# Moving the second half's weight loads ahead of the spill stores, with a lead of three steps

## The chip, the core and the metric

The kernel runs on one core of one Trainium2 chip. The metric is the device time of one execution in microseconds; the median of three runs is compared. A profile of a single execution, taken by the hardware profiler, goes with it. PE is the matmul engine (TensorE), PEld its weight loads, DVE is VectorE, ACT is ScalarE, POOL is GpSimd and SP is SyncE, the engine whose queue issues the DMAs here.

## The reference

One layer of a hybrid decoder, for one sequence of 1024 tokens and a model width of 2048, in float32. What matters for this change is its opening:

```python
mod = silu(c) @ w_ada + b_ada                   # w_ada: 2048 x 6144
shift, scale, gate = split(mod, 3)
h = rms_norm(x, norm_gain) * (1.0 + scale) + shift
proj = h @ w_in                                 # w_in: 2048 x 8192
q_sb, k_sb, v_sb, z_sb, q_r, k_r, v_r, z_r = split(proj)
# group A: stick-breaking attention on q_sb, k_sb, v_sb, times silu(z_sb)
# group B: chunkwise retention on rotary q_r, k_r and v_r, group norm, times silu(z_r)
out = x + gate * (concat(group A, group B) @ w_out)
```

Each group has 8 heads of 128. `mod` is itself a product of a vector with a matrix of 2048 x 6144, so w_ada has to be read as a whole.

## The kernel before

**Numbers.** A float32 factor is cut into a high part in a reduced format and the rest (`split`, `split_to`, lines 168 to 181: ACT writes the high part, DVE the low one). A product is then three matmuls (`mm3`, lines 183 to 186). PE is the engine that works all the time.

**The stages.** The opening (up to about 235 us) computes the modulation and the normed h, projects the retention queries `q_r` of seven heads with it, and builds from h the factors that the main products use. Then come the large products of h with the other columns of w_in, in blocks of a Winograd scheme, with the attention and retention of finished heads between them, and at last the product with w_out. The change is in the opening alone.

**The opening's two halves.** The sequence is cut into two halves of 512 tokens. Each half has 16 steps, one for each block of 128 rows of the model width. A step `p` of a half does, in the order in which PE is given it (`start_mm`, lines 717 to 725): for each of the 7 heads three matmuls that add the product of the step's weights and the step's h to that head's PSUM tile `first`. Between the heads stand, for later steps: the transposes of x (`x_turn`, 542), which fill a PSUM tile of tag `"C"` that ACT or DVE copies to `xT`; `make_h` (593), which makes the high and low part of h on ACT and DVE; `cut_w` (705), which cuts the next weights; `ada_sums` (563) and `ada_mod` (579), which work on one chunk of 256 columns of w_ada. Transposes, sums and mods all use the tag `"C"`, of which there is one buffer. So a transposed tile must have been copied out before a sum or a mod can start. The chunk numbers 8 to 15 of w_ada give `shift`.

In the second half step `p` transposes x and makes h for step `p + 2`, and cuts the weights of step `p + 2` at heads 4 and 6. In even steps it takes `ada_mod(cc)` at head 3, in odd steps `ada_sums(cc + 1)` at head 4, with `cc = 8 + p // 2`. From step 2 on, `factors` puts work on a list of which `pieces` gives a part after most heads to ACT and DVE: pieces `whole`, `high`, `minus`, `over`, `low` make factors `B22`, `T1`, `T2`, `T3`, `T4`, `B21` of two blocks k, and `low` stores the finished `B22`, `T1` and `T2` (high and low part, `store`, 359 to 362) to DRAM.

**Between the halves.** When the first half's products are done, `spill` (873) takes each head's `first` out of PSUM: DVE multiplies it with the row of norms, and SP stores it to `rqraw` (line 881). Seven heads make seven stores.

**The order of work.** From line 872 on every engine runs in the order in which the code issues; before it only PE does. All these DMAs are issued on SP, in order. A DMA that waits, for its data or for its buffer, holds all DMAs behind it.

**Buffers.** All tiles of 128 x 512 lie in 92 buffers, which `Slots` (57) gives out in turn: the buffer that was given back first is given out first. Giving back (`put`) happens in the code's order, so a tile may get a buffer whose last reader hasn't run yet; its writer then waits for that reader, or for the store that reads it.

**Loads.** `load_w(p, hf)` (696) issues two loads (128 x 512 and 128 x 384) for step `p`; `load_ada(cc)` (501) issues eight of 256 KB. In the first half, steps 14 and 15 load the weights of the second half's steps 0 and 1. In the second half, step `p` first issues the weights of step `p + 2`, and in even steps chunk `cc + 2` of w_ada; from step 12 on it also loads blocks of w_in for the next stage (`load_raw`, 254).

Of the kernel before, what the change touches and what calls it, by code (L numbers as in the profile page):

```python
# [20 lines left out]
KC = D // P  # L21
# [35 lines left out]
class Slots:  # L57
# [21 lines left out]
    def get(self, name, cls=None, dtype=F32, borrow=False):  # L79
        assert self.free, (name, cls, self.used)  # L80
        if cls in ("raw", "ring") and self.share and not (borrow or self.loose):
            assert self.used.get(cls, 0) < self.share[cls], (name, cls, self.used)
        i = self.free.popleft()
        self.used[cls] = self.used.get(cls, 0) + 1
        t = self.pool.tile([P, HALF], dtype, tag=f"s{i}", name=name)
        self.of[id(t)] = (t, i, cls)
        return t

    def put(self, *tiles):
        for t in tiles:  # L90
            _, i, cls = self.of.pop(id(t))
            self.used[cls] -= 1
            self.free.append(i)
# [3 lines left out]
def layer_kernel(ctx, tc, x, c, w_ada, b_ada, norm_gain, w_in, sb_q_gain, sb_k_gain, ret_norm_gain, w_out,  # L97
# [156 lines left out]
    def load_raw(gi, q, block, hh, borrow=False):  # L254
        col = groups[gi][q][0] + (P if block[1] == "2" else 0) if q < 4 else single
        kc = (8 if block[2] == "2" else 0) + 4 * hh
        t = raws[gi, q, block, hh] = get(f"{block}_{gi}_{q}_{hh}", "raw", borrow=borrow)
        nc.sync.dma_start(t.rearrange("p (k n) -> p k n", n=P), w_in_k[:, kc:kc + 4, col:col + P])
# [198 lines left out]
    def prepare_entry(j):  # L457
        if j < len(entries):
            lefts[j] = left(*entries[j])
        else:  # L460
            cut_left(j - len(entries))
# [39 lines left out]
    def load_ada(cc, gs=range(8)):  # L501

        col = (D + CHUNKS1[cc] * 2 * P) if cc < 8 else CHUNKS[cc - 8] * 2 * P
        for g in gs:
            ada[cc, g] = ar = get(f"ada_{cc}_{g}")
            nc.sync.dma_start(ar.rearrange("p (j n) -> p j n", n=2 * P),
                              ada_rows[:, 2 * g:2 * g + 2, col:col + 2 * P])
# [34 lines left out]
    def x_turn(p, g, tag, bufs):  # L542

        kc = (KCS if g else KCS1)[p]
        xT[kc, g] = get(f"xT{kc}_{g}")
        tp = ps.tile([P, HALF], F32, tag=tag, bufs=bufs, name=f"xtp_{kc}_{g}")
        for t in range(4):
            src = xt[4 * g + t, kc // 4]
            nc.tensor.transpose(tp[:, t * P:(t + 1) * P], src[:, (kc % 4) * P:(kc % 4 + 1) * P], ident)
        left_in[kc // 4, g] -= 1  # L550
        if left_in[kc // 4, g] == 0:
            put(*[xt.pop((4 * g + t, kc // 4)) for t in range(4)])
        if p % 2 and g == 0:
            nc.vector.tensor_copy(xT[kc, g], tp)
        else:
            nc.scalar.activation(xT[kc, g], tp, AF.Copy)
# [6 lines left out]
    def ada_sums(cc):  # L563


        ap_ = ps.tile([P, 256], F32, tag="C", name=f"accp_{cc}")
        for j in range(16):
            g = j % 4
            nc.tensor.matmul(ap_[32 * g:32 * g + 32, :], silu_z[:, j, :],  # L569
                             ada[cc, j // 2][:, (j % 2) * 256:(j % 2) * 256 + 256], start=j < 4, stop=j >= 12)  # L570
        put(*[ada.pop((cc, g)) for g in range(8)])
        acc = get(f"acc_{cc}")
        nc.vector.tensor_copy(acc[:, 0:256], ap_)
        return acc
# [4 lines left out]
    def ada_mod(cc, acc):  # L579

        mod = ps.tile([P, 2], F32, tag="C", name=f"mod_{cc}")
        for s in range(2):
            nc.tensor.matmul(mod[:, s:s + 1], acc[:, s * P:(s + 1) * P], ones[:, 0:1], start=True, stop=True)
        put(acc)
        k0 = 2 * (CHUNKS1[cc] if cc < 8 else CHUNKS[cc - 8])
        k2 = slice(k0, k0 + 2)
        if cc < 8:
            nc.vector.tensor_tensor(mods[:, k2], mod, scale_b1[:, k2], op=ALU.add)
            nc.vector.tensor_tensor(mods[:, k2], mods[:, k2], gain_c[:, k2], op=ALU.mult)
        else:  # L590
            nc.vector.tensor_tensor(shift[:, k2], mod, shift_b[:, k2], op=ALU.add)

    def make_h(p, hf):

        kc = (KCS if hf else KCS1)[p]
        a, xT_kc = mods[:, kc:kc + 1], xT[kc, hf]
        h_hi[kc, hf] = get(f"h_hi{kc}_{hf}", None, F32R)
        nc.scalar.activation(h_hi[kc, hf], xT_kc, AF.Copy, scale=a)
        h_lo[kc, hf] = get(f"h_lo{kc}_{hf}", None, F32R)
        nc.vector.scalar_tensor_tensor(h_lo[kc, hf], xT_kc, a, h_hi[kc, hf].bitcast(F32),  # L600
                                       op0=ALU.mult, op1=ALU.subtract)
# [85 lines left out]
    def pieces(n=1):  # L687
        for _ in range(n):
            if background:
                for fn in background.popleft():  # L690
                    if fn:
                        fn()
# [3 lines left out]
    def load_w(p, hf):  # L696
        raw = []
        for i in range(2):
            n = min(HALF, NZ * P - i * HALF)
            raw.append(get(f"wr_{p}_{hf}_{i}"))  # L700
            col, kc = rqcol + i * HALF, (KCS if hf else KCS1)[p]
            nc.sync.dma_start(raw[i][:, 0:n], w_in[0][kc * P:(kc + 1) * P, col:col + n])
        return raw

    def cut_w(p, hf, raw, i):
        return split(raw[i], f"first_{p}_{hf}_{i}", min(HALF, NZ * P - i * HALF))
# [10 lines left out]
    def start_mm(p, hf, ws, heads):  # L717
        kc = (KCS if hf else KCS1)[p]
        for h in heads:
            if p == 0:  # L720
                tag, bufs = starter_tags[h]
                first[h] = ps.tile([P, HALF], F32, tag=tag, bufs=bufs, name=f"first_{h}_{hf}")
            hi, lo = ws[h // 4]
            sl = slice(h % 4 * P, (h % 4 + 1) * P)
            mm3(first[h], hi[:, sl], lo[:, sl], h_hi[kc, hf], h_lo[kc, hf], p == 0, p == KC - 1)
# [96 lines left out]
    rawz = {}  # L822
# [50 lines left out]
    def spill(h, hf):  # L873
        zt = get(f"zt_{h}_{hf}")
        if hf == 0:
            nc.vector.tensor_tensor(zt, first[h], norm_row, op=ALU.mult)
        elif h % 2:
            nc.vector.tensor_copy(zt, first[h])
        else:
            nc.scalar.activation(zt, first[h], AF.Copy)  # L880
        nc.sync.dma_start(rqraw[h][:, halves(hf)], zt)
        put(zt)

    for h in range(NZ):
        spill(h, 0)

# [2 lines left out]
    def scale_some(n):  # L889
        for _ in range(min(n, len(unscaled))):  # L890
            t = xT[unscaled.popleft(), 0]
            nc.vector.tensor_tensor(t, t, norm_row, op=ALU.mult)
            if not unscaled:
                put(norm_row)

    early = deque([("A12", hh, q) for hh in range(2) for q in range(5)])
    for p in range(KC):
        cc = 8 + p // 2
        if p + 2 < KC:
            rawz[p + 2] = load_w(p + 2, 1)  # L900
        if p % 2 == 0 and cc + 2 < 16:
            load_ada(cc + 2)
        if p >= 12:
            for _ in range(3):
                if early:
                    b, hh, q = early.popleft()
                    load_raw(0, q, b, hh)
        w, cuts = ws.pop(p), []
        heads = range(NZ) if p < KC - 1 else (3, 0, 1, 2, 4, 5, 6)
        for i, h in enumerate(heads):  # L910
            start_mm(p, 1, w, (h,))
            if p == 1 and i or p > 1 and i < 2:
                scale_some(1)
            if i == 0 and p + 2 < KC:
                x_turn(p + 2, 1, "C", 1)
            if i == 2 and p + 2 < KC:
                make_h(p + 2, 1)
            if i == 3 and p % 2 == 0:
                ada_mod(cc, sums.pop(cc))
            if i == 4 and p % 2 and cc < 15:  # L920
                sums[cc + 1] = ada_sums(cc + 1)
            if i == 3 and p % 4 == 2:
                factors((KCS[p - 2], KCS[p - 1]))
            if i in (4, 6) and p + 2 < KC:
                cuts.append(cut_w(p + 2, 1, rawz[p + 2], i // 2 - 2))
            if i not in (2, 4):
                pieces()
            if p == KC - 1:
                if i:
                    spill(heads[i - 1], 1)  # L930
                if i in (1, 3, 5):
                    prepare_entry(i // 2)
        put(h_hi.pop((KCS[p], 1)), h_lo.pop((KCS[p], 1)))
        if p + 2 < KC:
            ws[p + 2] = cuts
            put(*rawz.pop(p + 2))
# [991 lines left out]
```

## Time and profile before

| | us |
|---|---|
| median of 3 runs | 1884.33 |
| lowest and highest run | 1883.38 and 1884.34 |
| the profiled execution | 1884.66 |
| its span, first to last instruction | 1882.9 |
| PE busy | 1866.6 |
| DVE busy | 1341.8 |
| ACT busy | 826.1 |

The span is what the profile's rows add up to; the time around it, 1.8 us, is not seen in them. All times in rows are counted from the start of the span. The granted clock of PE is full over the whole span. A row of a timeline has the start, the duration, the engine, the line of the code, the operation, what it writes and reads, and in brackets how long the engine was idle before it and what ended that. A row of a window has the stretch, its length, the busy time of PE, PEld, DVE, ACT and POOL with the number of instructions, PE's clock, the share in which the DMA engines were busy, and GB/s. A row of a wait has who waited for whom, the total, the number and the longest, and the row of landings gives the shortest, median and longest time from a DMA's issue to the arrival of its data. SPq is SP's queue.

### The profile page before, as it was taken

The numbers are of one execution on the slowest core, as the hardware profiler recorded it, in microseconds if no ns is written. First come the engines' busy times: TensorE is split into PE (matmuls) and PEld (weight loads), VectorE is DVE, ScalarE is ACT, GpSimd is POOL, SyncE is SP. The second block draws the span as 40 slices with busy tenths as digits, with TensorE's granted clock in tenths as the row PEclk, the third lists the DMA queues.
The fourth block names the chain that finished last, engine by engine and source line by source line (L and its number), as shares of the span: only waits on it lengthen the run. The fifth ranks groups of instructions, "written<-read, shape, count | busy, mean of one in ns | idle before, by whom it ended". The sixth has DMA issues, their size and how long they took to land.

```text
span 1882.9 us, 29009 instructions
## 1 busy us (share of the span) xinstructions
PE 1866.6 (99%) x9565; PEld 1540.5 (82%) x9565; DVE 1341.8 (71%) x2601; ACT 826.1 (44%) x1559; POOL 82.6 (4%) x278
## 2 busy tenths in 40 slices
PE   8999999999999999999999999999999999999998
PEld 5777788888888888888888888888888888888887
DVE  3568776666768677877688676977585666596669
ACT  3647762233544454445443554334334455342231
POOL 0000000000110010001010101000000000000000
PEclk9999999999999999999999999999999999999999
DMA  9979999998698789978997988999997963994594
GB/s 317 361 240 313 319 348 370 374 359 300 209 315 299 242 285 310 305 272 264 321 317 263 305 276 290 302 304 290 308 317 253 265 214 113 359 366 163 187 313 164
DMA packets 414451, 541.04 MB, mean 287 GB/s; under 512 B 34142, under 2 KB 210648, under 8 KB 414300
## 3 DMA queue, kind: packets, MB, share of 16 engines
q1 hardware_dynamic: 413436, 538.78, 86.9%
q8 instruction: 75, 1.23, 0.3%
q14 instruction: 76, 0.62, 0.1%
q10 hardware_dynamic: 864, 0.40, 0.1%
HBM read 453.03 MB, written 86.02 MB: 286 GB/s over the span
## 4 chain that ended last, share of the span: by engine, by line
PE 92%; DVE 4%; DMA 3%; issue 1%; ACT 0%; SPq 0%; DVEq 0%; ACTq 0%
PE pj L184 19%; PE pj L186 19%; PE pj L185 19%; PE y L185 5%; PE y L184 5%; PE y L186 5%; PE first L184 3%; PE first L186 2%; PE first L185 2%; PE accp L569 1%; PE tp_B L1248 1%; PE oT L184 1%; PE oT L186 1%; PE oT L185 1%; DMA ada<-in_w_ada_dram 1%; PE zp L186 1%
## 5 line engine op out<-in xcount | busy, mean ns | idle before, releaser
L173 DVE TENSOR_TENSOR wl<-A,wh 128x512 fp32r<-128x512 f32 x392 | 270.1, 690 | 211.5 <-ACT wh L171 198.1
L171 ACT ACTIVATE wh<-A 128x512 fp32r<-128x512 f32 x392 | 247.6, 632 | 387.0 <-PE pj L185 369.8
L387 ACT ACTIVATE c<-pj 128x512 f32<-128x512 f32 x112 | 66.7, 600 | 147.4 <-PE pj L186 137.4
L294 DVE TENSOR_TENSOR A<-A,A 128x512 f32<-128x512 f32 x160 | 110.0, 693 | 1.7
L390 DVE TENSOR_TENSOR c<-pj,c 128x512 f32<-128x512 f32 x112 | 74.9, 687 | 47.9 <-PE pj L186 47.5
L1212 ACT ACTIVATE om<-zp,y 128x128 f32<-128x128 f32 (+2 forms) x96 | 55.9, 582 | 107.4 <-PE zp L186 67.2
L184 PE MATMUL first<-h_hi,wh_first 128*128 128x512 f32 x224 | 94.6, 422 | 0.1
L1228 DVE TENSOR_TENSOR_SCAN om<-om 128x128 f32<-128x128 f32 (+2 forms) x96 | 93.5, 974 | 1.1
L184 PE MATMUL pj<-T1h,wh 128*128 128x512 f32 x232 | 94.2, 406 | 0.0
L184 PE MATMUL pj<-B22h,wh 128*128 128x512 f32 x232 | 92.8, 400 | 0.0
L184 PE MATMUL pj<-B21h,wh 128*128 128x512 f32 x232 | 92.0, 397 | 0.0
L184 PE MATMUL pj<-B11h,wh 128*128 128x512 f32 x232 | 91.4, 394 | 0.0
L186 PE MATMUL pj<-T1h,wl 128*128 128x512 f32 x232 | 90.7, 391 | 0.0
L186 PE MATMUL pj<-B22h,wl 128*128 128x512 f32 x232 | 90.6, 391 | 0.0
L185 PE MATMUL pj<-T1l,wh 128*128 128x512 f32 x232 | 90.5, 390 | 0.0
L185 PE MATMUL pj<-B21l,wh 128*128 128x512 f32 x232 | 90.5, 390 | 0.0
L186 PE MATMUL pj<-B21h,wl 128*128 128x512 f32 x232 | 90.4, 390 | 0.0
L186 PE MATMUL pj<-B11h,wl 128*128 128x512 f32 x232 | 90.4, 390 | 0.0
L185 PE MATMUL pj<-B11l,wh 128*128 128x512 f32 x232 | 90.4, 390 | 0.0
L185 PE MATMUL pj<-B22l,wh 128*128 128x512 f32 x232 | 90.4, 390 | 0.0
L184 PE MATMUL pj<-T3h,wh 128*128 128x512 f32 x224 | 89.6, 400 | 0.0
L184 PE MATMUL pj<-T4h,wh 128*128 128x512 f32 x224 | 89.5, 400 | 0.0
(411 smaller groups left out, 4963.2 us busy)
## 6 DMA issues: line engine op xcount, KB each, us to landing
A<-in_w_in_dram SPq DMA_DIRECT2D x228, 256.0 KB, 5.7
ada<-in_w_ada_dram SPq DMA_DIRECT2D x120, 256.0 KB, 5.6
wB<-in_w_out_dram SPq DMA_DIRECT2D x112, 256.0 KB, 5.3
gr<-in_w_ada_dram SPq DMA_DIRECT2D x64, 256.0 KB, 5.6
T2h<-fac_T SPq DMA_DIRECT2D x56, 256.0 KB, 5.4
T2l<-fac_T SPq DMA_DIRECT2D x56, 256.0 KB, 5.4
T1h<-fac_T SPq DMA_DIRECT2D x56, 256.0 KB, 5.4
T1l<-fac_T SPq DMA_DIRECT2D x56, 256.0 KB, 5.3
```

The lines of the kernel that those rows point to most:

```text
L171: nc.scalar.activation(hi[:, 0:n], src[:, 0:n], AF.Copy)
L173: nc.vector.tensor_tensor(lo[:, 0:n], src[:, 0:n], hi[:, 0:n].bitcast(F32), op=ALU.subtract)
L184: nc.tensor.matmul(o, a_hi, b_hi, start=first, stop=False, skip_group_check=on)
L185: nc.tensor.matmul(o, a_hi, b_lo, start=False, stop=False, skip_group_check=on)
L186: nc.tensor.matmul(o, a_lo, b_hi, start=False, stop=last, skip_group_check=on)
L294: nc.vector.tensor_tensor(r[o], r[a], r[b], op=ALU.add if n == 1 else ALU.subtract)
L387: nc.scalar.activation(t, o, AF.Copy)
L390: nc.vector.tensor_tensor(dst[q, cc], o, dst[q, cc], op=ALU.add)
L569: nc.tensor.matmul(ap_[32 * g:32 * g + 32, :], silu_z[:, j, :], ada[cc, j // 2][:, (j % 2) * 256:(j % 2) * 256 + 256], start=j < 4, stop=j ...
L1212: nc.scalar.activation(om[:, :n], zp[:, :n], AF.Sigmoid, scale=y[:, 16 + i:17 + i])
L1228: nc.vector.tensor_tensor_scan(rev, rev, rev, init, op0=ALU.mult, op1=ALU.bypass)
L1248: nc.tensor.transpose(banks_[j // 2][:, c0:c0 + P], be[:, j * P:(j + 1) * P], ident)
```

## The change

The loads of the second half's steps 2 and 3 and chunk 10 of w_ada are issued ahead of the seven spill stores of the first half, and the loop then issues the weights of step `p + 3` and, in odd steps, chunk `cc + 3`. Each of these loads stands one step earlier than before in SP's order. The number of loads, what they load, and all work of the other engines stay as they are; which of the 92 buffers a tile gets changes for the tiles of the second half.

```diff
@@ -881,6 +881,11 @@
         nc.sync.dma_start(rqraw[h][:, halves(hf)], zt)
         put(zt)
 
+
+    for p in (2, 3):
+        rawz[p] = load_w(p, 1)
+        if p == 2:
+            load_ada(10)
     for h in range(NZ):
         spill(h, 0)
 
@@ -896,10 +901,10 @@
     early = deque([("A12", hh, q) for hh in range(2) for q in range(5)])
     for p in range(KC):
         cc = 8 + p // 2
-        if p + 2 < KC:
-            rawz[p + 2] = load_w(p + 2, 1)
-        if p % 2 == 0 and cc + 2 < 16:
-            load_ada(cc + 2)
+        if p and p + 3 < KC:
+            rawz[p + 3] = load_w(p + 3, 1)
+        if p % 2 and cc + 3 < 16:
+            load_ada(cc + 3)
         if p >= 12:
             for _ in range(3):
                 if early:
```

## The prediction

> **What bounds the kernel now.** I read the page first: the busy times of the engines.
>
> ```profile
> span 1882.9 us, 29009 instructions
> PE 1866.6 (99%) x9565; PEld 1540.5 (82%) x9565; DVE 1341.8 (71%) x2601; ACT 826.1 (44%) x1559; POOL 82.6 (4%) x278
> ```
>
> PE is busy for all but 16.3 us of the span. An edit that moves loads takes no matmul away, so it can win only what PE idles, and only where those loads are the cause. The next view is therefore the list of PE's waits, first for 0 to 240 us, then for the rest of the span.
>
> ```profile
> PE xtp L549 <- DMA x<-in_x_dram: 3.3, 7, 0.9
> PE mod L583 <- ACT xT L556: 1.6, 1, 1.6
> ```
>
> ```profile
> PE tp_B L1248 <- DVE al L1273: 0.9, 3, 0.4
> ```
>
> The columns are total, times and longest, in us. The waits for x lie in the first half, which the change doesn't touch, and those at L1248 lie after 500 us, in attention. One wait lies in the opening's second half: 1.6 us before the products of ada_mod. The timelines of PE, ACT and DVE around it say why.
>
> ```profile
> 139.34 0.60 PE L549 MATMUL xtp<-ident,x 128*128 128x128 f32 x4
> ...
> 141.61 0.39 PE L186 MATMUL first<-h_hi,wl_first 128*128 128x512 f32 x1
> 143.60 0.61 PE L583 MATMUL mod<-ones,acc 128*128 128x1 f32 x4 [1.61 <-ACT xT L556]
> ```
>
> ```profile
> 137.96 0.42 DVE L573 COPY acc<-accp 128x256 f32<-128x256 f32 x1
> ```
>
> ```profile
> 140.66 0.63 ACT L171 ACTIVATE wh_first<-wr 128x512 fp32r<-128x512 f32 x1 [5.04 <-DMA wr<-in_w_in_dram]
> 142.54 0.52 ACT L171 ACTIVATE wh_first<-wr 128x384 fp32r<-128x384 f32 x1 [1.24 <-DMA wr<-in_w_in_dram]
> 142.97 0.58 ACT L556 ACTIVATE xT<-xtp 128x512 f32<-128x512 f32 x1
> ```
>
> This is step p=2. Its transposes (139.34) go into the only PSUM buffer of tag C. ada_mod of the same step needs that buffer, so it needs ACT's copy xT. ACT works in order, and ahead of that copy stand the two cuts of the weights for step 3, which wait for their load until 142.5. So the load is the cause. Why it is late is in SyncE's timeline, its wait list and the windows.
>
> ```profile
> 105.18 2.47 SPq L702 DMA_DIRECT2D wr<-in_w_in_dram  x4
> 121.97 6.86 SPq L881 DMA_DIRECT2D rqraw<-zt  x7
> ...
> 129.92 4.22 SPq L506 DMA_DIRECT2D ada<-in_w_ada_dram  x8
> 134.51 2.74 SPq L702 DMA_DIRECT2D wr<-in_w_in_dram  x4
> 137.51 6.63 SPq L506 DMA_DIRECT2D ada<-in_w_ada_dram  x8
> ```
>
> ```profile
> SPq L881 <- DVE zt L876: 18.0, 7, 13.9
> ```
>
> ```profile
> 112.00:122.00 10.00, 10.00 (x74) 7.42 (x73) 4.20 (x8) 3.21 (x6) 0.00 (x0) 1.00 0.01 2
> 129.00:147.00 18.00, 16.39 (x103) 12.43 (x103) 9.26 (x18) 6.07 (x11) 0.00 (x0) 1.00 1.05 336
> ```
>
> ```profile
> DMA to landing us min/median/max: 6.0/6.6/7.1
> ```
>
> SyncE issues the loads of steps 0 and 1 until 107.65, then stands 13.9 us at the first spill store, which waits for DVE, which waits for the end of the first half on PE. Behind it stand the loads of steps 2 and 3. In 112 to 122 us the DMA engines are 1% busy; from 129 on they are full at 336 GB/s, and the weights of steps 3 and 4 (issued from 134.51) take 6.0 to 7.1 us to land, which is the last row.
>
> **The change part by part.** *The loads ahead of the stores.* Twelve loads (4 of weights, 8 of w_ada) move past the seven stores. They now follow 107.65 directly, if their buffers are free. Slots hands out 92 buffers from a queue, first freed, first used again. I walked its gets and puts in the order of the code, with the moved loads in their new places. The twelve then get buffers last used by squares of x, by chunk 7 of w_ada and by h of step 12.
>
> ```profile
> 102.78 1.93 PE L569 MATMUL accp<-ada,silu_z 128*32 128x256 f32 x32
> ```
>
> ```profile
> 104.06 0.62 ACT L514 ACTIVATE junk<-x 128x512 f32<-128x512 f32 x1
> ```
>
> The two named readers are done by 104.7, and step 12 of the first half ends before its successor's transposes, around 109. At the slowest pace of the rows above (6.63 us for eight, 0.83 each) the twelve are issued by 117.6 and landed by 124.7. The stores, due at 121.97, are not delayed: 4.3 us of cover. Were it gone, SyncE alone would be late: nothing in the opening reads what they store, and their buffers come round again only in step 3's loads. Step 3's weights are first cut about 135, so ACT waits for neither cut, copies xT at about 139.9 to 140.5, and ada_mod's acc is there at 138.4. PE ends the matmul before at 142.0, so nothing is late and **the 1.61 us go**. I find no second wait behind: 1.5 us lie between that copy and PE's need.
>
> *Three steps' lead in the loop.* No load is added; each stands one step earlier in SyncE's program. Between 129 and 146 us the engines stay full as now, but each weight tile is now issued a step or more ahead of its cut. After 144 PE waits for nothing in this stretch, so an earlier load gains nothing more.
>
> *What it costs.* Ten buffers more (2 + 8) are held during odd steps. By the walk the queue's lowest filling in steps 7 to 11 goes from 12 to 9, and in step 9 from 19 to 9. Buffers are used again sooner. From step 14 on every get falls on the same predecessor as before, so all that comes after the opening is unchanged. And in steps 7 and 9 ten loads now stand in SyncE's program ahead of stores of factors that stood ahead of them: T2 of k=1 in step 7; T1 and T2 of k=2 in step 9. Who waits for those stores? By the walk, in step 8, ACT's T2h and DVE's B22l take the two buffers of T2 of k=1. In step 10, DVE's T2 takes the buffer of T1h, ACT's T3h that of T1l, ACT's h_hi that of T2h, DVE's h_lo that of T2l. Behind h_lo on DVE stands `shift`, which frees the buffer C for the transposes of step 11. The rows:
>
> ```profile
> 161.35 1.87 SPq L702 DMA_DIRECT2D wr<-in_w_in_dram  x4
> 163.28 4.24 SPq L506 DMA_DIRECT2D ada<-in_w_ada_dram  x8
> ...
> 174.05 0.32 SPq L361 DMA_DIRECT2D fac_T<-T1l  x1
> ...
> 185.93 0.34 SPq L361 DMA_DIRECT2D fac_B<-B22l  x1
> ...
> 187.33 0.38 SPq L360 DMA_DIRECT2D fac_T<-T1h  x1
> ...
> 188.88 0.98 SPq L361 DMA_DIRECT2D fac_T<-T2l  x1
> 189.95 1.50 SPq L702 DMA_DIRECT2D wr<-in_w_in_dram  x2
> 191.50 4.84 SPq L506 DMA_DIRECT2D ada<-in_w_ada_dram  x8
> ```
>
> ```profile
> DMA to landing us min/median/max: 4.4/4.8/5.2
> ```
>
> ```profile
> 184.18 0.62 ACT L608 ACTIVATE T2h<-T 128x512 fp32r<-128x512 f32 x1
> ```
>
> ```profile
> 185.21 0.68 DVE L615 TENSOR_TENSOR B22l<-xT,B22h 128x512 fp32r<-128x512 f32 x1
> ...
> 194.47 0.69 DVE L641 TENSOR_TENSOR T<-xT,xT 128x512 f32<-128x512 f32 x1
> ...
> 195.82 0.75 DVE L600 SCALAR_TENSOR_TENSOR h_lo<-xT,mods,h_hi 128x512 fp32r<-128x512 f32 x1
> 196.49 0.15 DVE L591 TENSOR_TENSOR shift<-mod,cols 128x2 f32<-128x2 f32 x1
> ```
>
> ```profile
> 199.16 0.60 PE L549 MATMUL xtp<-ident,x 128*128 128x128 f32 x4
> ```
>
> These are SyncE's timeline, the landing of stores, and the timelines of ACT, DVE and PE. The landing row is that of the four fac_T stores of 187.33 to 188.88. Ten loads take 5.1 us (161.35 to 167.52 is twelve) to 6.3 us (189.95 to 196.34 is ten). All engine times below are 1.6 us earlier than the rows.
>
> Step 7: T1l is issued at 172.45, ten loads end at 177.9 to 179.1, the T2 stores land 4.7 later, T2h at 182.6 to 183.8, T2l half a us after. ACT wants T2h's buffer at 182.6 and DVE the other at 183.6: waits of 0 to 1.2 and 0 to 0.7 us, in front of no PE need. They may delay B22l's store by some 0.4 us.
>
> Step 9: B22l's store at 184.3 + 0.4, ten loads from 185.1, so T1h at 190.2 to 191.4, T2l 1.55 later (187.33 to 188.88) at 191.8 to 192.95, landed at 196.2 to 198.15, middle 197.2. DVE meets its first such wait at 192.9 and can start h_lo only at 197.2; shift ends 0.83 later (195.82 to 196.64), at 198.0. PE's transposes are due at 197.55. So PE waits 0.5 us, between 0 and 1.4, and up to 2.0 with step 7's delay whole. h_lo itself is needed only in step 12, some 6 us on; wl for step 12 then comes at about 199.5, also in time. I take 0.5.
>
> The fixed price of a store is where a page speaks. The Trainium skill, DMA: Bandwidth & Descriptors, section Anatomy of one DMA, fits a transfer on the GpSimd path as 2.0 us plus its bytes over 436 GB/s; for 256 KB that is an estimate of 2.6 us, and by it the T2l store would land by 195.6, before anyone is late. The trace agrees only for stores on empty queues, the first row here, not for those behind loads:
>
> ```profile
> DMA to landing us min/median/max: 2.0/2.0/2.0
> ```
>
> These are the seven spill stores; 4.4 to 5.2 us, the row above, is the nearer case.
>
> **Sum.** -1.6 + 0.5 = -1.1 us. The profiled execution took 1884.66 us, its span and 1.8 around it, and would take 1883.55; it lies 0.3 above the median of the three runs, 1884.33, so the median should be about 1883.2. About 0.2% (3.8 us) is what a measurement of this kernel can tell from no change; the whole gain at stake is below half of that.
>
> **The rivals.** *Nothing is given back.* The delayed stores land on nearly idle queues, in the spill stores' 2.0 us: T2l at 193.8 to 195, and h_lo finds its buffer free. Then the whole 1.6 stays: 1882.7. For it: the stores come at the end of ten loads, with none behind. Against it: the four stores at 187.33 had a similar load burst before them and took 4.4 to 5.2. The fit cited above would have it so.
>
> *Slower: the recycled buffers in step 10.* If the ten loads go at the full queue's 0.75 us (134.51 to 137.51 is four) and the stores behind them take the 7.1 us of step 3's weights, T2l is issued at 185.7 + 7.5 + 1.55 = 194.75 and lands at 201.85; shift ends at 202.7, and PE's transposes wait 5.1 us: a net +3.5, 1887.8. It decides against the change once T2l lands after 198.3, for then the wait passes 1.6. For it: DVE, ACT and SyncE are all in order and chained here. Against it: the burst of step 9 starts on a queue that holds only two stores and two loads.
>
> *The lead does nothing.* If a buffer of the twelve is held longer than I counted, SyncE stops there and the loads leave after the stores as now, or another ACT task takes the place of the cuts: 1884.3. Against it: all three kinds of readers end before 109.
>
> **How the numbers follow.** The forecast, 55%; nothing given back, 25%; slower, 12%; no effect, 8%. The runs shown spread over 1.0 us, half of which I add below 1882.7, and a little: low 1882.0. Above, no effect and the cheaper part of the slower case reach 1885.5. Faster by over 0.2% needs 3.8 us, which PE doesn't idle here: 0.02. Slower by over 0.2% needs a wait of 5.4 us, the far end of the slower case and what I may have missed: 0.05. The rest, 0.93.
>
> **What would show it.** In the profile after: twelve loads on SyncE right after 107.65 and ahead of the L881 stores; DMA busy in 112 to 122; no wait of PE at L583 near 142; PE's second half ending 1 to 1.6 us earlier. Of the cost: SyncE's T1 and T2 stores of k=2 after an eight-load row of w_ada near 190, DVE idle before `T` of L641 near 193 and before h_lo near 197, and a PE wait at xtp near 198 on DVE's shift of about 0.5 us. The forecast is wrong if PE shows several waits above 1 us between 145 and 225, or if anything differs after 240 us.

## The result, and the profile after

The changed kernel is slower: a median of 1890.11 us (1888.98 to 1892.34, 6 runs) against 1883.94 us (1883.18 to 1884.34, 6 runs), a ratio of 1.0031 with a 95% interval of 1.0021 to 1.0041. The forecast of 1883.2 with its range to 1885.5 was wrong. The page of the changed kernel's profile begins so:

```profile
span 1888.8 us, 29030 instructions
PE 1868.8 (99%) x9565; PEld 1543.2 (82%) x9565; DVE 1341.4 (71%) x2601; ACT 824.9 (44%) x1559; POOL 82.1 (4%) x278
```

The span is 5.9 us longer with as many matmuls, and PE is busy 2.2 us longer. PE's waits between 100 and 235 us (who waited for whom, total, times, longest):

```profile
PE xtp L549 <- DVE shift L591: 5.6, 1, 5.6
```

The 1.6 us at ada_mod are gone, as forecast. In their place stands one wait, at the place where the forecast had put one of 0.5 us. First the part that worked, SyncE's timeline and the DMA engines at the border of the halves:

```profile
106.52 3.90 SPq L702 DMA_DIRECT2D wr<-in_w_in_dram  x6
110.86 4.59 SPq L506 DMA_DIRECT2D ada<-in_w_ada_dram  x8
115.80 1.08 SPq L702 DMA_DIRECT2D wr<-in_w_in_dram  x2
122.03 6.86 SPq L881 DMA_DIRECT2D rqraw<-zt  x7
```

```profile
112.00:122.00 10.00, 10.00 (x73) 7.42 (x72) 4.20 (x8) 3.27 (x6) 0.00 (x0) 1.00 0.90 298
```

The twelve loads leave by 116.9 in the gap that was empty (DMA share 0.90 where it was 0.01), and the stores begin at 122.03, as before. Now step 9 on SyncE, and what follows on DVE, ACT and PE:

```profile
186.42 0.33 SPq L361 DMA_DIRECT2D fac_B<-B22l  x1
186.84 0.88 SPq L702 DMA_DIRECT2D wr<-in_w_in_dram  x2
187.81 4.50 SPq L506 DMA_DIRECT2D ada<-in_w_ada_dram  x8
192.40 0.46 SPq L360 DMA_DIRECT2D fac_T<-T1h  x1
193.64 0.34 SPq L361 DMA_DIRECT2D fac_T<-T1l  x1
...
195.08 0.32 SPq L361 DMA_DIRECT2D fac_T<-T2l  x1
```

```profile
DMA to landing us min/median/max: 7.8/7.8/7.8
```

```profile
185.70 0.69 DVE L615 TENSOR_TENSOR B22l<-xT,B22h 128x512 fp32r<-128x512 f32 x1 [2.17 <-DMA fac_T<-T2l]
...
200.33 0.69 DVE L641 TENSOR_TENSOR T<-xT,xT 128x512 f32<-128x512 f32 x1 [7.13 <-DMA fac_T<-T1h]
...
202.98 0.15 DVE L591 TENSOR_TENSOR shift<-mod,cols 128x2 f32<-128x2 f32 x1
```

```profile
185.13 0.63 ACT L608 ACTIVATE T2h<-T 128x512 fp32r<-128x512 f32 x1 [2.61 <-DMA fac_T<-T2h]
...
200.93 0.63 ACT L608 ACTIVATE T3h<-T 128x512 fp32r<-128x512 f32 x1 [8.04 <-DMA fac_T<-T1l]
201.56 0.72 ACT L598 ACTIVATE h_hi<-xT,mods 128x512 fp32r<-128x512 f32 x1
```

The landing (issue to arrival) is that of the T1h store, the one of the four whose arrival the profile shows: issued at 192.40 behind ten loads, landed at 200.2. DVE's `T` takes its buffer and waits 7.13 us, ACT's `T3h` takes that of T1l and waits 8.04. Behind them, in order, stand h_hi on ACT, then h_lo and shift on DVE; PE gets the PSUM buffer at 203.1. PE's own timeline shows the rest of the loss:

```profile
197.16 0.39 PE L186 MATMUL first<-h_hi,wl_first 128*128 128x512 f32 x1
203.19 1.12 PE L549 MATMUL xtp<-ident,x 128*128 128x128 f32 x4 [5.64 <-DVE shift L591]
...
205.38 0.63 PE L184 MATMUL first<-h_hi,wh_first 128*128 128x512 f32 x1
205.81 0.63 PE L185 MATMUL first<-h_lo,wh_first 128*128 128x512 f32 x1
206.24 0.62 PE L186 MATMUL first<-h_hi,wl_first 128*128 128x512 f32 x1
...
206.93 0.39 PE L185 MATMUL first<-h_lo,wh_first 128*128 128x512 f32 x1
207.16 0.39 PE L186 MATMUL first<-h_hi,wl_first 128*128 128x512 f32 x1
```

```profile
200.00:206.00 6.00, 2.81 (x9) 2.43 (x10) 4.98 (x10) 5.07 (x10) 0.00 (x0) 0.50 0.19 70
```

From 203.2 to 206.7 matmuls start 0.43 us apart instead of 0.23; in the window's row, the granted clock is 0.50. Set against the kernel before, instruction by instruction, PE is 1.7 us early from 142 on, 4.0 us late at the transposes of step 11 (203.19 against 199.16), and 5.7 us late once the clock is back: **1.7 us won, 5.7 lost in the wait, 1.7 lost at half clock**. After that the difference moves by 0.3 us at most to the end.

### The profile page after: what moved, and what is told of

It reads as the page before. It is cut to its first block, busy times and chain, and to the rows that moved or that the text cites. A ratio compares the mean times of both kernels' runs of the same rounds, so it can differ in the third digit from the quotient of the medians.

```text
span 1888.8 us, 29030 instructions
## 1 busy us (share of the span) xinstructions
PE 1868.8 (99%) x9565; PEld 1543.2 (82%) x9565; DVE 1341.4 (71%) x2601; ACT 824.9 (44%) x1559; POOL 82.1 (4%) x278
## 4 chain that ended last, share of the span: by engine, by line
PE 91%; DVE 4%; DMA 3%; issue 1%; ACT 0%; SPq 0%; ACTq 0%; DVEq 0%
PE pj L184 19%; PE pj L186 19%; PE pj L185 19%; PE y L184 5%; PE y L185 5%; PE y L186 5%; PE first L184 3%; PE first L186 2%; PE first L185 2%; PE accp L569 1%; PE tp_B L1253 1%; DMA ada<-in_w_ada_dram 1%; PE oT L184 1%; PE oT L186 1%; PE oT L185 1%; PE zp L186 1%
```

## The experiments

Theory: the T1 and T2 stores of k=2 stand behind ten loads on SyncE, and step 10 takes their buffers again, so the in-order chain store, DVE, shift, PSUM buffer, PE waits for a landing. Rivals: the early loads as such, by filling the DMA engines; the short queue of free buffers alone; step 7's delay as the trigger. Ratios are to the kernel before, run on the same chip. The diffs are against the changed kernel and leave helper lines out; the line numbers in a run's rows are those of its own kernel.

**Only the loads ahead of the stores.**

```diff
-        if p and p + 3 < KC:
-            rawz[p + 3] = load_w(p + 3, 1)
-        if p % 2 and cc + 3 < 16:
-            load_ada(cc + 3)
+        if p > 1 and p + 2 < KC:
+            rawz[p + 2] = load_w(p + 2, 1)
+        if p and p % 2 == 0 and cc + 2 < 16:
+            load_ada(cc + 2)
```

> Only the twelve loads go ahead of the spill stores; in the loop the lead stays at two steps. Theory (the loss is the T1 and T2 stores of k=2 standing behind ten loads in step 9, with their buffers taken again in step 10): PE's wait of 1.6 us at ada_mod near 142 is gone, none comes near 199, the time is 1.6 us below the kernel before, some 1882.3. Rival (loading early itself does the harm, by filling the DMA engines ahead of stores): slower than before, above 1885.

1882.80 us against 1884.10, ratio 0.9994 (0.9985 to 1.0003). In its profile PE waits for nothing between 47 and 500 us. The early loads do no harm; the gain is of the forecast size, and the interval doesn't part it from none.

**Only the lead of three steps.** The hoisted loads stand behind the spill stores again:

```diff
+    for h in range(NZ):
+        spill(h, 0)
     for p in (2, 3):
         rawz[p] = load_w(p, 1)
         if p == 2:
             load_ada(10)
-    for h in range(NZ):
-        spill(h, 0)
```

> Only the lead of three steps: the twelve loads are issued behind the spill stores as before. Theory: the two parts add up, so the 1.6 us at ada_mod near 142 stay and the loss near 199 stays: 1890.1 + 1.7 = 1891.8. Rival (the loads ahead of the stores are what crowds the queue in step 9): less than 1886.

1891.19 us, ratio 1.0035 (1.0022 to 1.0049). Its PE waits between 100 and 235 us:

```profile
PE xtp L549 <- DVE shift L591: 5.2, 1, 5.2
PE mod L583 <- ACT xT L556: 0.7, 1, 0.7
```

The loss belongs to the longer lead alone. The old wait is back, at 0.7 instead of 1.6 us.

**The same order, other buffers.** `defer`, a method added to `Slots`, moves named free buffers to the end of the queue:

```diff
+        if p == 10:
+            slots.defer(("T1h_2", "T1l_2", "T2h_2", "T2l_2"))
         if p and p + 3 < KC:
             rawz[p + 3] = load_w(p + 3, 1)
```

> The whole change, SyncE's order as in it, but at step 10 the four buffers of T1h, T1l, T2h and T2l of k=2 go to the end of the queue of free buffers, so that step 10 takes others. Theory: the stores still go out near 192.4 and land late, near 200, but nobody in step 10 waits for them: the 7 to 8 us waits of DVE at T and of ACT at T3h go, PE has no wait near 199 and keeps its clock: 1882.3 to 1882.6. Rival (full DMA engines delay step 10 whatever buffers it takes): PE's wait stays above 3 us, the time above 1886.

1882.57 us, ratio 0.9993 (0.9984 to 1.0001). Its SyncE timeline, landing of the T1h store, and DVE:

```profile
186.62 3.97 SPq L516 DMA_DIRECT2D ada<-in_w_ada_dram  x8
190.68 0.55 SPq L370 DMA_DIRECT2D fac_T<-T1h  x1
```

```profile
DMA to landing us min/median/max: 6.5/6.5/6.5
```

```profile
192.20 0.69 DVE L651 TENSOR_TENSOR T<-xT,xT 128x512 f32<-128x512 f32 x1
...
194.22 0.15 DVE L601 TENSOR_TENSOR shift<-mod,cols 128x2 f32<-128x2 f32 x1
```

The store still leaves behind ten loads and lands at 197.2, but `T` runs at 192.20 without a wait and `shift` at 194.22. Full DMA engines don't delay step 10; taking these buffers does.

**The same buffers, the old order.** Chunk 15 takes its buffers in step 9 (`hold_ada` gets the eight, without a load) and is issued in step 10:

```diff
-        if p % 2 and cc + 3 < 16:
+        if p == 9:
+            hold_ada(15)
+        elif p == 10:
+            load_ada(15)
+        elif p % 2 and cc + 3 < 16:
             load_ada(cc + 3)
```

> The whole change, but chunk 15 of w_ada takes its eight buffers in step 9 and is issued only in step 10: the same buffers come round in step 10, while the T1 and T2 stores of k=2 have only two loads ahead of them. Theory: these stores go out near 188 to 190 and land within 4 to 5 us, by 194.5, so DVE waits about 1 us instead of 7.1 and PE 0 to 0.5 us: 1882.3 to 1883. Rival (the short queue of free buffers alone does it): PE still waits above 3 us, 1886 or more.

1882.82 us, ratio 0.9993 (0.9984 to 1.0002). SyncE, and the landing:

```profile
186.18 0.88 SPq L707 DMA_DIRECT2D wr<-in_w_in_dram  x2
187.15 0.38 SPq L360 DMA_DIRECT2D fac_T<-T1h  x1
...
188.62 0.68 SPq L361 DMA_DIRECT2D fac_T<-T2l  x1
```

```profile
DMA to landing us min/median/max: 3.3/3.3/3.3
```

With two loads ahead instead of ten, the same store leaves 5.2 us sooner and lands in 3.3 us. DVE and ACT wait for no store of k=2. So both are needed, the order and the recycled buffers, and taking away either restores the gain.

**The stores past SyncE.** GpSimd issues the T1 and T2 stores of k=1 and k=2:

```diff
-        nc.sync.dma_start(fac[n, k][:, 0], hi.bitcast(F32))
-        nc.sync.dma_start(fac[n, k][:, 1], lo.bitcast(F32))
+        q = nc.gpsimd if n in ("T1", "T2") and k in (1, 2) else nc.sync
+        q.dma_start(fac[n, k][:, 0], hi.bitcast(F32))
+        q.dma_start(fac[n, k][:, 1], lo.bitcast(F32))
```

> The whole change, with the T1 and T2 stores of k=1 and k=2 issued by GpSimd instead of SyncE, so that they don't stand behind loads in SyncE's order; loads, buffers and their order stay. Theory (SyncE's order holds the stores back): T1 and T2 of k=2 go out when they are ready, near 186, and land before 193; DVE and ACT wait at most 1 us, PE not at all near 198: 1882.5. Rival (the DMA engines, full of w_ada's loads, hold the stores back whoever issues them): they land after 196, PE waits above 2 us, 1885 or more.

1883.13 us, ratio 0.9995 (0.9986 to 1.0004). GpSimd's timeline, and the landing of the last three stores:

```profile
182.65 0.54 POOL L361 DMA_DIRECT2D fac_T<-T1h  x1 [8.12 <-ACT T1h L609]
...
187.04 0.54 POOL L362 DMA_DIRECT2D fac_T<-T2l  x1
```

```profile
DMA to landing us min/median/max: 5.4/6.7/7.0
```

Beside the loads they too take 5.4 to 7.0 us. But they leave when they are ready, the last at 187.04, and these three are there by 194.0. The engines' load makes landings long; SyncE's order made the issue late.

**Step 7 undone.** Chunk 14 is loaded in step 8 again, so the T2 stores of k=1 aren't held back:

```diff
-        if p % 2 and cc + 3 < 16:
+        if p % 2 and cc + 3 < 16 and cc != 11:
             load_ada(cc + 3)
+        if p == 8:
+            load_ada(14)
```

> The whole change, but chunk 14 of w_ada is loaded in step 8 as before; chunk 15 stays early in step 9. So the T2 stores of k=1 have only two loads ahead of them. Theory (step 9 makes the wait, step 7 adds about 2 us to it): the waits of ACT at T2h and DVE at B22l near 183 go, the T1 store of k=2 goes out near 190.4 and lands at 197 to 198, PE waits 2 to 3.5 us at xtp near 198: 1884.5 to 1887. Rival (step 7's delay is the trigger, without it the stores are in time): no wait of PE near 198, 1882.5.

1886.93 us, ratio 1.0012 (1.0003 to 1.0021). The time is inside the theory's range. PE waits 1.58 us in the profiled execution, less than expected, and keeps its clock behind it; such a wait only cancels the 1.6 us won, so the loss of the median is not seen in this one profile. By the times step 9 alone still costs, and step 7 makes it worse.

**The load behind the stores.** Step 13's weights leave one step later:

```diff
-        if p and p + 3 < KC:
+        if p and p + 3 < KC and p != 10:
             rawz[p + 3] = load_w(p + 3, 1)
+        if p == 11:
+            rawz[13] = load_w(13, 1)
```

> The whole change, but the weights of step 13, which stand right behind the T1 and T2 stores of k=2, are loaded one step later. Theory (the stores are late because of what is ahead of them in the queue): the T1 store still takes 6.5 to 7.8 us to land, PE's wait stays at 5 to 5.6 us, 1890. Rival (what is issued behind the stores takes DMA time from them): the T1 store lands a microsecond or more sooner, PE's wait shrinks to 4 to 4.5, 1888 to 1889.

1889.43 us, ratio 1.0028 (1.0019 to 1.0038); landing 6.3 us, wait 3.4. The landing fits the rival, the wait is below its 4 to 4.5 us, and the time lies above its 1889; but the changed kernel itself, in a later profile (below), has 6.2 and 3.9. The edit also moves the buffers on by two, so T1h's goes to B21l. The runs don't settle this.

**What the clock costs.** PE gets 24 matmuls of noughts to do while it would wait (`nought` is a tile of zeros that ACT writes before the second half):

```diff
+            if i == 0 and p == 11:
+                for _ in range(24):
+                    nc.tensor.matmul(first[6], nought, h_hi[KCS[p], 1], start=False, stop=False, skip_group_check=True)
```

> The whole change, with 24 matmuls of a tile of noughts into a PSUM tile that they leave as it is, put on PE ahead of the transposes of step 11, so that PE is busy (24 x 0.23 = 5.5 us) while it would wait for shift. Theory (of the loss, 5.6 us are the wait and about 1.7 us the halved clock after it): the transposes start as late as in the changed kernel, but the matmuls behind them keep 0.23 us: 1.7 us less than the changed kernel, 1888.4. Rival (the slow matmuls after the wait have another cause, such as late operands): 1890.

1888.46 us, ratio 1.0023 (1.0014 to 1.0032). PE's timeline:

```profile
196.54 5.61 PE L923 MATMUL first<-h_hi,nought 128*128 128x512 f32 x24
201.99 0.60 PE L549 MATMUL xtp<-ident,x 128*128 128x128 f32 x4
...
202.89 0.40 PE L186 MATMUL first<-h_hi,wl_first 128*128 128x512 f32 x1
```

The transposes follow the noughts at once, at 201.99; `shift` ends at 201.81 here, so without the noughts PE would have waited some 5 us. The matmuls behind them stay at 0.39 us. Since this interval overlaps that of the changed kernel, three kernels ran side by side.

> The changed kernel itself, beside the two below on one chip. Theory: as measured before, near 1890, with a wait of PE of 4 to 6 us at xtp near 198 and slow matmuls behind it; the landing of the T1 store of k=2 varies from run to run (6.0 to 7.8 us so far) and the wait with it.

> The kernel of e7_busy_wait beside the changed kernel on one chip. Theory (the halved clock costs 1.7 us): 1.5 to 1.9 us less than e10_change. Rival (no such cost): the same time within 0.5 us.

> As e7_busy_wait, with 12 matmuls of noughts instead of 24, so that PE idles 2.2 to 3 us behind them. Theory (the clock falls only after an idle time longer than the 1.6 us that left it full and at most as long as the 3.4 us that halved it in e8_load13_back): I expect the clock to hold, and a time of 1888.4, as with 24. Rival (any idle time above 2 us halves it): 1889.5 to 1890.

The changed kernel took 1889.56 us (ratio 1.0027, 1.0019 to 1.0036), with 24 matmuls 1888.28 (1.0021, 1.0012 to 1.0030), with 12 matmuls 1888.03 (1.0021, 1.0012 to 1.0030). The medians lie 1.3 us (24, short of the 1.5 to 1.9 expected) and 1.5 us (12) below the change; the intervals overlap, so the size rests on the traces. The changed kernel's PE timeline, and that with 12 matmuls:

```profile
200.86 0.72 PE L549 MATMUL xtp<-ident,x 128*128 128x128 f32 x4 [3.95 <-DVE shift L591]
...
203.09 0.63 PE L185 MATMUL first<-h_lo,wh_first 128*128 128x512 f32 x1
```

```profile
201.20 0.66 PE L549 MATMUL xtp<-ident,x 128*128 128x128 f32 x4 [1.39 <-DVE shift L591]
...
202.62 0.39 PE L185 MATMUL first<-h_lo,wh_first 128*128 128x512 f32 x1
```

In this profile of the changed kernel (1888.07 us, its fastest execution here) the wait is 3.95 us. From the transposes of step 11 to those of step 12 PE then needs 8.98 us (200.86 to 209.84), where the kernel before needs 7.33 (199.16 to 206.49): the half clock costs 1.65 us. With 12 matmuls, 1.39 us of idleness were left (less than the 2.2 to 3 expected), the clock held, and the same stretch took 7.38 us.

No version was clearly better than the kernel before: the four that lose PE's wait lie at 0.9993 to 0.9995, each with an interval that reaches 1.

## Why the prediction was wrong

**The step that failed** is the price of step 9's stores. The prediction had them landed by 198.15 and PE waiting 0.5 us; they landed so late that PE waited 5.64 us, and behind that wait 1.7 us more went at half clock, a cost for which the sum had no term.

**Right.** PE's one wait in this stretch, its cause and its end came as written. So did the place of the price and the engines on its path: the stores of k=2, `T` and T3h in step 10, h_lo, shift, the transposes of step 11, with the first waits in step 8. One link was another: the forecast let h_lo wait for T2l's landing. In the trace the last wait for a store is T3h's for T1l (until 200.93); h_lo then waited only for ACT's h_hi. After the opening nothing moved by more than 0.3 us.

**Wrong: four terms of that chain, and what I made of the "slower" rival.**

- *Step 7's waits.* Priced at 0 to 1.2 us with 0.4 passed on; they were 2.61 (ACT) and 2.17 (DVE). B22l's store left at 186.42, not at 184.7. Undoing step 7 took the ratio from 1.0031 to 1.0012.
- *The issue of the stores behind the burst.* T1h at 192.40, where 190.2 to 191.4 was written; T2l 2.7 us behind it, not 1.55: between the four, SyncE waited 1.3 us for landings of w_ada.
- *Their landing.* 7.8 us against 4.4 to 5.2. The row I took was of stores with two loads ahead of them. With ten ahead the T1 store took 6.0 to 7.8 us over the profiles, with two 3.3 where chunk 15 was put back. This is the largest error, about 3 us here and 1.4 in the later profile (6.2 us), and the row of the weights that took 6.0 to 7.1 us was the nearer one. The cited fit of 2.0 us plus bytes, an estimate of 2.6 us, holds for none of these stores, and the spill stores' 2.0 us lie 0.6 below it.
- *The clock.* The sum had no term for what a long wait does afterwards: 1.7 us. The profile before could not show it in this stretch, since its wait of 1.6 us left the clock full.

The sum should have been -1.6 + 5.6 + 1.7 = +5.7. The rival had nearly the wait (5.1 us) and gave it 12%, with the argument that the burst starts on a queue that is nearly empty. By the landings, 7.8 us behind ten loads and 3.3 behind two, that looked at the wrong end: how full the queue is when the burst is over counts for more. That 5.1 comes so near 5.64 is in part luck, for the rival too had T2l as the last store waited for, and its burst begins 0.6 us later than the forecast's (185.7 against 185.1) without a row for it. Its time, 1887.8, ended just below the 0.2% bound, and so "slower" got 0.05; with the clock's 1.7 us it would have been 1889.5, close to what was measured.

The clock's rule stands in the Trainium skill, TensorE: Matmul & The Clock Gate, section Part 1: The HAM clock gate: after an idle window of about 3.4 us PE goes to half rate, and it needs about as long of work to come back. The traces agree in the main: single waits of 1.39, 1.58 and 1.61 us left it full, 3.36, 3.95, 5.24 and 5.64 us halved it, for 3.4 us after the first two of these and for 6.8 us after the others.

But the traces show no length below which a wait is safe. Near 36 us, in the first half, which the change doesn't touch, the clock fell to 0.50 for 3.4 us in three of the thirteen profiles (only the loads ahead of the stores, step 7 undone, and the second run with 24 matmuls) after four waits for x of at most 0.48 us each within 2.4 us. It cost each some 1.5 us, as much as the change could win: from the last of those transposes to the chunk sums near 52 us it took them 16.9 to 17.0 us, the kernel before 15.4. The other ten had waits of like size there and kept the clock.

## What to carry to other kernels

A longer lead on an in-order DMA queue is paid by the stores that the loads now stand ahead of. Look up who next takes each store's buffer, and price that store's landing by rows taken behind an equally full queue. In these traces a wait of PE of 3.4 us or more cost some 1.7 us beyond itself, and a single one of 1.6 us or less nothing; so a bound on a long wait needs the clock added. Where an early load and a recycled buffer meet, moving either is enough: other buffers, the store's old place, or another queue for the store.

## What the runs showed of the hardware

A 256 KB store took 2.0 us to land on empty queues, 3.3 to 5.7 with two loads directly ahead of it and 5.4 to 7.8 with ten. The number of loads alone doesn't fix it: the T2 store of k=1 took 5.7 us behind two with step 7 undone and 5.6 behind ten in the changed kernel. Issued from GpSimd beside the same loads such stores took 5.4 to 7.0: another queue spares the place in the order, not the load on the engines.
